# Which loads lie among the first MLP unit's weight tiles, and in which order its splits run: a decoder block on one core

## The chip, the core and the metric

One core of a Trainium2 chip runs one decoder block for 256 tokens of width 2048, in float32. The metric is the device time of one launch, in microseconds (us): the median of several runs.

## What is computed

The block is an adaptive-norm decoder layer. Six vectors of 2048 come from the conditioning vector and are used as shifts, scales and gates; two branches (a state-space one and an attention one) are merged, and an MLP follows. The end of it matters here:

```python
mod = silu(c) @ w_ada + b_ada                     # 12288 columns
sh1, sc1, g1, sh2, sc2, g2 = split(mod, 6)
...
x  = x + g1 * (merged @ w_out)
h2 = rms_norm(x, norm_mlp_g) * (1 + sc2) + sh2
x  = x + g2 * (square(relu(h2 @ w_ff1)) @ w_ff2)
return rms_norm(x, norm_final_g)
```

The weights (w_out 2048 x 2048, w_ff1 2048 x 8192, w_ff2 8192 x 2048, w_ada 2048 x 12288) are each read once.

## The kernel before, in words

**Products in three parts.** Every float32 weight tile (128 x 1024, 512 KB) is loaded into a raw buffer, `wraw`, of which there are seven, and then split in two: ScalarE (ACT in the profile) casts it to `hi` (line 137) and VectorE (DVE) computes `lo = raw - hi` (line 139). The activations are split in the same way. TensorE (PE) then does three matmuls for each product: hi by hi, hi by lo, lo by hi. There are four buffers each for `whi` and `wlo`; a few units write their splits into other large buffers that are free just then ("homes": `wVT`, `wQT` and so on). A raw buffer is free for the next load once VectorE has done the `lo` part.

**Engines and queues.** Each engine works through its own list in order, and all the loads concerned are issued by one queue, SyncE's (SP), in order as well. The order on each engine is set when the program is built, by a scheduler that goes by priorities and by extra edges: `self.after(ins)` puts what is issued inside it behind `ins`, when both are on the same engine. The lists `self.gates` and the values `self.gate` and `self.hgate` do this for the next weight tiles: an entry holds the instruction on VectorE behind which the `lo` part of a tile goes and the one on ScalarE behind which its cast goes. `turns` does it for matmuls: from a given tile on, the first product of a token half goes behind a given transpose.

**w_ada on VectorE.** Most of the product with w_ada isn't done on TensorE. A transposed tile of w_ada is loaded into a raw buffer (line 316), and VectorE multiplies it by the broadcast conditioning vector and sums it up (line 323, a "total"); after eight of these there are four columns' worth of 128 values. Such jobs wait in a lane, `ada`: after each weight tile that the program streams, the lane is credited its rate, and when a whole credit is there one job is issued (the load of one tile and the total of the one before). The constant `RM` is that rate for the section described next, and `self.agate`, when it is set, puts the totals behind the instruction it holds.

**The place of the change.** The second half of `w_out` (columns 1024 on) is done for tokens 0 to 127 first, then for tokens 128 to 255 ("halves" t = 0 and 1). Each half has its norm chain, `norm2(t)`: the gated result is added to x (lines 1159 and 1160), its squares are summed on ScalarE (line 1161), the sum goes through a square root on ScalarE (line 394) and a few one-column instructions on VectorE to the scaling of the row (line 1172, `xs`); TensorE transposes it (`trh`), ScalarE applies scale and shift (line 1193, `htmp`, one buffer), and the split makes `mh`. This is done for the two first quarters of the columns (c = 0 and 1) in turn; the other two follow later.

While the second half of the norm isn't done, the MLP starts with what there is. Four *units* (g = 0 to 3) form the products of the first half of the columns (K tiles 0 to 7) with 1024 columns of w_ff1 each, and keep them as `part`. The first unit, `gemm_h` with eight tiles, does all tiles for tokens 0 to 127 and then all for tokens 128 to 255, so that the second norm chain can run under the first; its tiles 4 to 7 go to `wVT` (two) and `wQT` (two). The units 1 to 3 are done in two runs of four tiles (`gemm_w`, 512 columns and two K tiles a load, line 179). Then the eight MLP groups follow (`ff1`, `ff2`), where the other K tiles are added.

Before the change, the lane's rate is 0.72 from the first unit on. The totals among the first unit's tiles are put behind `h1`, the last split of the second norm chain. The lo parts of tiles 1 to 3 go behind the first scaling of the first norm chain (`scaled[0]`), and the first half's matmuls of tile 7 go behind the second chain's last transpose.

Of the kernel before, what the change touches and what calls it, by code (L numbers as in the profile page):

```python
# [55 lines left out]
RSS = .43  # L56
RPA = .65
RWO = .45
RM = .72
NP = 4  # L60
TW = 9
TF = 3
# [12 lines left out]
class Kern:  # L75
# [776 lines left out]
    def body(self):  # L852
# [263 lines left out]
        for b in range(4):  # L1116
            t = sg[:, b]
# [53 lines left out]
            o, i_ = xs[:, t, c * 512:(c + 1) * 512], x1[:, t, c * 512:(c + 1) * 512]  # L1171
            return v.tensor_scalar(o, i_, rs2[t], None, op0=OP.mult)

        scaled = {}

        def norm2(t):
            add1(t)
            with self.hot():
                ss = self.col(f"ss2{t}", 1)
                self.pin(v.reduce_sum(ss, sq[:, 4 * t:4 * t + 4], axis=AX.X))  # L1180
                rs2[t] = self.rstd(ss, 1, f"r2{t}")
                tk = slice(t * P, (t + 1) * P)
                scaled[t] = [scale2(c, t) for c in range(2)][0]
                for c in range(2):
                    p = self.tmp("trh")
                    h = self.big.tile([P, 4, P], F32, name="htmp", tag="htmp", bufs=1)
                    for k in range(4):
                        kt = 4 * c + k
                        self.turned[2 * t + c] = nc.tensor.transpose(
                            p[:, k * P:(k + 1) * P], xs[:, t, kt * P:(kt + 1) * P], self.ident)  # L1190
                    for k in range(4):
                        kt = 4 * c + k
                        nc.scalar.activation(h[:, k], p[:, k * P:(k + 1) * P], AF.Identity,
                                             scale=A2[:, kt:kt + 1], bias=B2[:, kt:kt + 1])
                    last = self.split(mh[:, 4 * c:4 * c + 4, tk], ml[:, 4 * c:4 * c + 4, tk], h)
            return last

        norm2(0)
        next(parts)
        h1 = norm2(1)  # L1200
        self.agate = h1
        self.gates = [(None, None)] + [(scaled[0], None)] * 3

        g2b = self.slot("S3", [P, D], name="g2b")

# [80 lines left out]
                            final(t)  # L1286

        parts = []
        self.lanes["ada"][1] = RM
        for g in range(NP):  # L1290
            part = self.slot(("S4", "T", "SV", "S5")[g], [P, 8, S], name="part")
            if g == 0:
                halves = self.gemm_h(w1, range(0, 8), 0, mh, ml, self.homes(4, ("VT", "QT")), 8,
                                     turns=(((7, 3),), ()))
                for t in range(2):
                    banks = next(halves)
                    for b in (2 * t, 2 * t + 1):
# [5 lines left out]
                    v.tensor_add(part[:, 4 * i + b], part[:, 4 * i + b], banks[b][:, 0:S])  # L1303
            parts.append(part)
            if g == 0:
                self.agate = None
                self.gates = []
                with self.after(h1):
                    for c in (2, 3):
                        for t in range(2):  # L1310
# [61 lines left out]
```

## Time and profile before

| | us |
|---|---|
| median of 3 runs | 1423.72 |
| the three runs | 1422.74 to 1424.9 |
| the profiled execution, its own time | 1423.38 |
| its span, first to last instruction | 1421.6 |
| TensorE busy in the span | 1375.3 |
| VectorE busy | 1055.3 |
| ScalarE busy | 705.2 |

The granted clock of TensorE is 0.989 of full speed on average. A line of the timeline gives the start in us from the span's start, the duration, the engine, the line of the program, the operation and its output and inputs; in brackets stands for how long the engine was idle before it and what ended that. Matmuls are pipelined, so that starts lie closer together than the durations say. In a table by stage, "x" counts instructions, and the column behind the engines is TensorE's granted clock.

### The profile page before, as it was taken

The page shows a single profiled execution, that of the slowest core. Times are in us where ns is not written, and L with a number is a line of the kernel's source. Part 1 is how long each engine was busy: PE and PEld are TensorE (multiplying, and loading weights), DVE is VectorE, ACT ScalarE, POOL GpSimd, SP SyncE. Part 2 cuts the span into 40 slices and gives each one's busy share as a digit, 9 for nine tenths or more (in the row PEclk, how much of TensorE's full clock was granted, in tenths as well). Part 3 has the DMA queues.
Part 4 walks back from the last instruction along what each step waited for, and adds up shares of the span by engine and source line. Part 5 has one row for each costly group of instructions (what it writes and reads, how often), then busy time and mean ns, then how long its engine had stood idle before and what let it go on. Part 6 is the DMA issues. An engine that isn't in the chain of part 4 may idle for free.

```text
span 1421.6 us, 23396 instructions
## 1 busy us (share of the span) xinstructions
PE 1375.3 (97%) x9258; PEld 1222.9 (86%) x9258; DVE 1055.3 (74%) x1502; ACT 705.2 (50%) x937; POOL 40.9 (3%) x94
## 2 busy tenths in 40 slices
PE   7799999999999999999899999999999999999996
PEld 6789899899999999988678888888888888888885
DVE  5688999986799888978686675777666555555676
ACT  4444353357464853445555564545463544634444
POOL 1000000320000300000000000000000000000000
PEclk9899999999999999999999999999999999999998
DMA  8999987597457988797497577777767556465551
GB/s 336 353 385 348 314 306 244 164 286 251 150 189 250 309 315 295 285 349 283 160 320 246 186 260 250 235 254 292 251 220 267 184 188 194 175 208 190 181 205 61
DMA packets 113293, 353.19 MB, mean 248 GB/s; under 512 B 12080, under 2 KB 12096, under 8 KB 113056
## 3 DMA queue, kind: packets, MB, share of 16 engines
q1 hardware_dynamic: 110384, 347.13, 70.4%
q0 software_dynamic: 2800, 4.58, 1.1%
q8 instruction: 72, 1.18, 0.3%
q14 instruction: 37, 0.30, 0.1%
HBM read 347.27 MB, written 2.29 MB: 246 GB/s over the span
## 4 chain that ended last, share of the span: by engine, by line
PE 85%; DMA 6%; DVE 5%; ACT 2%; issue 2%; SPq 0%; DVEq 0%; ACTq 0%
PE pw L198 14%; PE pn L268 10%; PE pn L267 10%; PE pn L269 10%; PE pt L170 9%; PE pt L172 9%; PE pt L171 9%; PE pw L200 7%; DMA wraw<-in_w_in_dram 2%; DMA wraw<-in_w_ff_dram 2%; DVE wraw L323 2%; DVE wlo L139 1%; DMA wraw<-in_w_out_dram 1%; ACT whi L137 1%; PE ss L409 1%
## 5 line engine op out<-in xcount | busy, mean ns | idle before, releaser
L137 ACT CAST whi<-wraw 128x1024 fp32r<-128x1024 f32 x443 | 461.3, 1050 | 553.2 <-PE pn L268 179.9
L139 DVE TENSOR_TENSOR wlo<-wraw,whi 128x1024 fp32r<-128x1024 f32 x443 | 537.7, 1221 | 260.4 <-ACT whi L137 257.0
L198 PE MATMUL pw<-mh,whi 128*128 128x512 f32 x896 | 311.4, 396 | 1.6 <-ACT part L1298 0.7
L170 PE MATMUL pt<-ah,whi 128*128 128x256 f32 x896 | 252.2, 289 | 10.4 <-ACT whi L137 5.4
L171 PE MATMUL pt<-ah,whi 128*128 128x256 f32 x896 | 250.4, 285 | 0.0
L200 PE MATMUL pw<-mh,wlo 128*128 128x256 f32 x896 | 242.2, 280 | 2.3 <-DVE wlo L139 2.3
L172 PE MATMUL pt<-ah,wlo 128*128 128x256 f32 x896 | 239.1, 286 | 4.3 <-DVE wlo L139 4.2
L323 DVE SCALAR_TENSOR_TENSOR wraw<-wraw,cb 128x1024 f32<-128x1024 f32 x176 | 213.0, 1217 | 0.0
L268 PE MATMUL pn<-whi,ff 128*128 128x512 f32 x512 | 199.3, 389 | 0.0
L198 PEld LDWEIGHTS pw<-mh,whi 128*128 128x128 f32 x896 | 165.6, 188 | 38.3 <-ACT part L1298 1.1
L267 PE MATMUL pn<-whi,ff 128*128 128x512 f32 x512 | 198.4, 390 | 0.0
L170 PEld LDWEIGHTS pt<-ah,whi 128*128 128x128 f32 x896 | 172.3, 194 | 14.5 <-ACT whi L137 7.6
L269 PE MATMUL pn<-wlo,ff 128*128 128x512 f32 x512 | 184.6, 389 | 0.0
L200 PEld LDWEIGHTS pw<-mh,wlo 128*128 128x128 f32 x896 | 168.9, 188 | 7.6 <-DVE wlo L139 3.3
L171 PEld LDWEIGHTS pt<-ah,whi 128*128 128x128 f32 x896 | 172.8, 193 | 0.3
L172 PEld LDWEIGHTS pt<-ah,wlo 128*128 128x128 f32 x896 | 165.6, 193 | 6.2 <-DVE wlo L139 6.0
L267 PEld LDWEIGHTS pn<-whi,ff 128*128 128x128 f32 x512 | 96.1, 188 | 20.2 <-issue 0.2
L269 PEld LDWEIGHTS pn<-wlo,ff 128*128 128x128 f32 x512 | 96.0, 188 | 19.8
L268 PEld LDWEIGHTS pn<-whi,ff 128*128 128x128 f32 x512 | 96.2, 188 | 19.6
L1273 DVE TENSOR_TENSOR y<-y,pn 128x512 f32<-128x512 f32 x48 | 30.8, 682 | 14.1 <-PE pn L269 14.1
L267 PE MATMUL pn<-whi,mh 128*128 128x512 f32 x96 | 37.6, 392 | 0.0
L268 PE MATMUL pn<-whi,mh 128*128 128x512 f32 x96 | 37.4, 390 | 0.0
(400 smaller groups left out, 1657.4 us busy)
## 6 DMA issues: line engine op xcount, KB each, us to landing
wraw<-in_w_ff_dram SPq DMA_DIRECT2D x256, 512.0 KB, 4.8
wraw<-in_wat_dram SPq DMA_DIRECT2D x176, 512.0 KB, 5.7
wraw<-in_w_in_dram SPq DMA_DIRECT2D x128, 512.0 KB, 5.3
wraw<-in_w_out_dram SPq DMA_DIRECT2D x32, 512.0 KB, 6.3
wraw<-in_wan_dram SPq DMA_DIRECT2D x16, 512.0 KB, 8.5
wraw<-in_w_proj_attn_dram SPq DMA_DIRECT2D x16, 512.0 KB, 6.6
wraw<-in_w_proj_ssm_dram SPq DMA_DIRECT2D x16, 512.0 KB, 6.3
wraw<-in_w_glu_dram SPq DMA_DIRECT2D x8, 512.0 KB, 5.5
```

The costliest lines, as they stand in the source:

```text
L137: h = self.nc.scalar.copy(hi, src)
L139: s = self.nc.vector.tensor_sub(lo, src, hi.bitcast(F32))
L170: nc.tensor.matmul(o, hi[:, c], xh[:, kx, :], start=st, stop=False, skip_group_check=True)
L171: nc.tensor.matmul(o, hi[:, c], xl[:, kx, :], start=False, stop=False, skip_group_check=True)
L172: self.mm = nc.tensor.matmul(o, lo[:, c], xh[:, kx, :], start=False, stop=sp, skip_group_check=True)
L198: nc.tensor.matmul(banks[b], hi[:, c], x2[:, k0 + k].rearrange("p h s -> p (h s)"), start=i + k == 0, stop=False, skip_group_check=True)
L200: self.mm = nc.tensor.matmul(banks[b][:, 0:S], lo[:, c], x2[:, k0 + k, 0, :], start=False, stop=i == n - 1 and k == 1, skip_group_check=True)
L267: nc.tensor.matmul(o, xh[:, kx, tk], hi[:, c], start=q == 0, stop=False)
L268: nc.tensor.matmul(o, xl[:, kx, tk], hi[:, c], start=False, stop=False)
L269: self.mm = last = nc.tensor.matmul(o, xh[:, kx, tk], lo[:, c], start=False, stop=q == n - 1)
L323: v.scalar_tensor_tensor(w, w, 1.0, self.cb[:, (i % 2) * 1024:(i % 2 + 1) * 1024], op0=OP.mult, op1=OP.mult, accum_out=pc[:, i:i + 1])
L1273: v.tensor_add(d, d, banks[b])
```

## The change

Three numbers and two lists change, all within the section from the second norm to the fourth unit.

- The lane's rate is zero while the first unit's tiles are streamed, so that its eight loads follow one another. After the unit, six jobs of the lane are issued at once, with their totals behind `h1`; then the rate is 0.45 (before 0.72), so that ten more are spread over units 1 to 3.
- The gates of the first unit's tiles: the lo parts of tiles 1 to 5 go behind the first scaling of the first chain, and those of tiles 6 and 7 behind the last split of that chain (`h0`); the casts of tiles 3 to 7 go behind the first chain's square root (`roots[0]`).
- `turns`: the first half's matmuls go behind the second chain's last transpose from tile 6 on (before from tile 7 on).

```diff
-RM = .72
+RM = .45
...
-        scaled = {}
+        scaled, roots = {}, {}
...
                 rs2[t] = self.rstd(ss, 1, f"r2{t}")
+                roots[t] = self.sq_last
...
-        norm2(0)
+        h0 = norm2(0)
         next(parts)
         h1 = norm2(1)
-        self.agate = h1
-        self.gates = [(None, None)] + [(scaled[0], None)] * 3
+        self.gates = [(None, None)] + [(scaled[0], None)] * 2 + [(scaled[0], roots[0])] * 3 + [(h0, roots[0])] * 2
...
-        self.lanes["ada"][1] = RM
+        self.lanes["ada"][1] = 0.0
...
-                                     turns=(((7, 3),), ()))
+                                     turns=(((6, 3),), ()))
...
             if g == 0:
+                self.gates = []
+                self.agate = h1
+                for job in range(6):
+                    if self.lanes["ada"][0]:
+                        self.lanes["ada"][0].pop(0)()
                 self.agate = None
-                self.gates = []
+                self.lanes["ada"][1] = RM
```

What this moves is seen in the order of the instructions on each engine. Names carry a running number of the buffer's use. The first place is the loads on SyncE's queue, from the first unit's first tile on; before:

```order
L132 DMA wraw_7751<-in_w_ff1_dram 128x1024
L316 DMA wraw_7763<-in_wat_dram 128x1024
L132 DMA wraw_7766<-in_w_ff1_dram 128x1024
L132 DMA wraw_7778<-in_w_ff1_dram 128x1024
L316 DMA wraw_7790<-in_wat_dram 128x1024
L132 DMA wraw_7793<-in_w_ff1_dram 128x1024
L316 DMA wraw_7805<-in_wat_dram 128x1024
L132 DMA wraw_7808<-in_w_ff1_dram 128x1024
L132 DMA wraw_7819<-in_w_ff1_dram 128x1024
L316 DMA wraw_7829<-in_wat_dram 128x1024
L132 DMA wraw_7832<-in_w_ff1_dram 128x1024
L316 DMA wraw_7843<-in_wat_dram 128x1024
```

and now:

```order
L132 DMA wraw_7751<-in_w_ff1_dram 128x1024
L132 DMA wraw_7763<-in_w_ff1_dram 128x1024
L132 DMA wraw_7775<-in_w_ff1_dram 128x1024
L132 DMA wraw_7787<-in_w_ff1_dram 128x1024
L132 DMA wraw_7799<-in_w_ff1_dram 128x1024
L132 DMA wraw_7810<-in_w_ff1_dram 128x1024
L132 DMA wraw_7820<-in_w_ff1_dram 128x1024
L132 DMA wraw_7831<-in_w_ff1_dram 128x1024
L316 DMA wraw_7893<-in_wat_dram 128x1024
L316 DMA wraw_7896<-in_wat_dram 128x1024
L316 DMA wraw_7899<-in_wat_dram 128x1024
L316 DMA wraw_7902<-in_wat_dram 128x1024
```

The tiles of w_ff1 (line 132) stood two and one between w_ada tiles (line 316); now all eight come first and the w_ada tiles follow.

The second place is the first norm chain on ScalarE. `whi`, `wVT` and `wQT` are casts of the first unit's tiles, r20s is the square root, L1161 the squares; before:

```order
L137 CAST whi_7780<-wraw_7778 128x1024
L1161 ACTIVATE xs_6984,sq_6985<-x_6983 128x512 x2
L137 CAST whi_7795<-wraw_7793 128x1024
L394 ACTIVATE r20s_7609<-r20v_7608 128x1
L1193 ACTIVATE htmp_7620<-trh_7619,B2_115,A2_114 128x128 x4
L137 CAST mh_6424<-htmp_7620 128x4x128
L137 CAST wVT_7810<-wraw_7808 128x1024
L1193 ACTIVATE htmp_7632<-trh_7631,B2_115,A2_114 128x128 x4
```

and now (line 1194 is line 1193 before):

```order
L137 CAST whi_7777<-wraw_7775 128x1024
L1161 ACTIVATE xs_6984,sq_6985<-x_6983 128x512 x2
L394 ACTIVATE r20s_7609<-r20v_7608 128x1
L137 CAST whi_7789<-wraw_7787 128x1024
L137 CAST wVT_7801<-wraw_7799 128x1024
L137 CAST wVT_7801<-wraw_7810 128x1024
L137 CAST wQT_7822<-wraw_7820 128x1024
L1194 ACTIVATE htmp_7620<-trh_7619,B2_115,A2_114 128x128 x4
L137 CAST mh_6424<-htmp_7620 128x4x128
L137 CAST wQT_7822<-wraw_7831 128x1024
L1194 ACTIVATE htmp_7632<-trh_7631,B2_115,A2_114 128x128 x4
```

The root stood behind the cast of the fourth tile; now it stands ahead of it, and three more casts are done before the first chain's htmp.

On VectorE the same stretch, from the first chain's scaling to the second chain's add; before:

```order
L1172 TENSOR_SCALAR xs_6984<-x_6983,r20s_7609 128x512 x2
L139 TENSOR_TENSOR wlo_7769<-wraw_7766,whi_7768 128x1024
L139 TENSOR_TENSOR wlo_7781<-wraw_7778,whi_7780 128x1024
L139 TENSOR_TENSOR wlo_7796<-wraw_7793,whi_7795 128x1024
L139 TENSOR_TENSOR mh_6424<-htmp_7620,mh_6424 128x4x128
L139 TENSOR_TENSOR wVT_7810<-wraw_7808,wVT_7810 128x1024
L139 TENSOR_TENSOR wVT_7810<-wraw_7819,wVT_7810 128x1024
L139 TENSOR_TENSOR mh_6424<-htmp_7632,mh_6424 128x4x128
L1159 TENSOR_TENSOR xs_6984<-pn2_7351,g1b_7068 128x512
L1160 TENSOR_TENSOR x_6983<-x_6983,xs_6984 128x512
L1159 TENSOR_TENSOR xs_6984<-pn3_7352,g1b_7068 128x512
```

and now:

```order
L1172 TENSOR_SCALAR xs_6984<-x_6983,r20s_7609 128x512 x2
L139 TENSOR_TENSOR wlo_7766<-wraw_7763,whi_7765 128x1024
L139 TENSOR_TENSOR wlo_7778<-wraw_7775,whi_7777 128x1024
L139 TENSOR_TENSOR wlo_7790<-wraw_7787,whi_7789 128x1024
L139 TENSOR_TENSOR wVT_7801<-wraw_7799,wVT_7801 128x1024
L139 TENSOR_TENSOR wVT_7801<-wraw_7810,wVT_7801 128x1024
L139 TENSOR_TENSOR mh_6424<-htmp_7620,mh_6424 128x4x128
L139 TENSOR_TENSOR mh_6424<-htmp_7632,mh_6424 128x4x128
L1159 TENSOR_TENSOR xs_6984<-pn2_7351,g1b_7068 128x512
L139 TENSOR_TENSOR wQT_7822<-wraw_7820,wQT_7822 128x1024
L139 TENSOR_TENSOR wQT_7822<-wraw_7831,wQT_7822 128x1024
L1160 TENSOR_TENSOR x_6983<-x_6983,xs_6984 128x512
```

Five tile splits now stand between the scaling and the first `mh` split, where three did, and two more between the second chain's first multiply (L1159) and its add (L1160).

The third place is TensorE around the second chain's transposes, at the end of the first unit's first half; before:

```order
L229 MATMUL pn1_7748<-wVT_7810,mh_6424 128x512
L230 MATMUL pn1_7748<-wVT_7810,mh_6424 128x512
L228 MATMUL pn0_7747<-wQT_7834,mh_6424 128x512
L229 MATMUL pn0_7747<-wQT_7834,mh_6424 128x512
L228 MATMUL pn1_7748<-wQT_7834,mh_6424 128x512
L229 MATMUL pn1_7748<-wQT_7834,mh_6424 128x512
L230 MATMUL pn0_7747<-wQT_7834,mh_6424 128x512
L230 MATMUL pn1_7748<-wQT_7834,mh_6424 128x512
L1189 MATMUL trh_7716<-ident_85,xs_6984 128x128 x4
L1189 MATMUL trh_7728<-ident_85,xs_6984 128x128 x4
```

and now:

```order
L229 MATMUL pn1_7748<-wVT_7801,mh_6424 128x512
L230 MATMUL pn1_7748<-wVT_7801,mh_6424 128x512
L1190 MATMUL trh_7716<-ident_85,xs_6984 128x128 x4
L1190 MATMUL trh_7728<-ident_85,xs_6984 128x128 x4
L228 MATMUL pn0_7747<-wQT_7822,mh_6424 128x512
L229 MATMUL pn0_7747<-wQT_7822,mh_6424 128x512
L230 MATMUL pn0_7747<-wQT_7822,mh_6424 128x512
L228 MATMUL pn1_7748<-wQT_7822,mh_6424 128x512
L229 MATMUL pn1_7748<-wQT_7822,mh_6424 128x512
L230 MATMUL pn1_7748<-wQT_7822,mh_6424 128x512
```

The six matmuls of tile 6 (the first `wQT` tile) stood ahead of the transposes and now stand behind them. In units 1 to 3 on VectorE, a total (line 323) stood behind almost every split until the lane was empty, in the third unit's first run for instance as split, total, split, total, split, total; now it is split, total, split, split, total, and totals go on to the fourth unit.

## The prediction

> **What bounds the kernel now.** I read the page first, then the busy time by stage, then the chain of waits and the timelines of the stage that the edit touches. The page gives the span; the stages show where TensorE is not busy (columns: time, then PE, PEld, DVE, ACT, POOL busy, granted clock, DMA).
>
> ```profile
> span 1421.6 us, 23396 instructions
> 667.00:684.00 17.00, 14.88 (x71) 12.19 (x70) 13.96 (x24) 9.29 (x14) 0.00 (x0) 1.00 0.79 299
> 684.00:708.00 24.00, 21.95 (x90) 16.70 (x89) 14.52 (x24) 14.32 (x30) 0.00 (x0) 0.93 0.47 154
> 708.00:735.00 27.00, 25.61 (x139) 21.33 (x138) 25.90 (x43) 13.22 (x20) 0.00 (x0) 1.00 0.92 325
> 735.00:760.00 25.00, 22.43 (x126) 18.86 (x125) 17.38 (x26) 10.45 (x16) 0.00 (x0) 1.00 0.80 262
> 760.00:800.00 40.00, 40.00 (x232) 34.95 (x231) 23.43 (x33) 21.96 (x33) 0.00 (x0) 1.00 0.63 204
> ```
>
> TensorE is idle for 2.12 + 2.05 + 1.39 + 2.57 = 8.1 us between 667 and 760 and for nothing from 760 to 800: the stage from the second norm to the third MLP unit is the only one here with anything to win. Its idle ends, and the clock, in order:
>
> ```profile
> 680.23 0.39 PE L230 MATMUL pn<-wSV,mh 128*128 128x512 f32 x1
> 682.73 1.07 PE L1189 MATMUL trh<-ident,xs 128*128 128x128 f32 x8 [2.12 <-DVE xs L1172]
> 683.55 0.49 PE L228 MATMUL pn<-wS,mh 128*128 128x512 f32 x1
> 683.50:687.20 3.70, 3.70 (x12) 0.55 0.51 151
> 689.37 0.62 PE L228 MATMUL pn<-whi,mh 128*128 128x512 f32 x2
> 698.43 0.61 PE L230 MATMUL pn<-wQT,mh 128*128 128x512 f32 x2
> 699.97 1.06 PE L1189 MATMUL trh<-ident,xs 128*128 128x128 f32 x8 [0.92 <-DVE xs L1172]
> 701.14 0.50 PE L228 MATMUL pn<-wQT,mh 128*128 128x512 f32 x1
> 704.09 0.73 PE L228 MATMUL pn<-whi,mh 128*128 128x512 f32 x2 [0.96 <-ACT mh L137]
> 704.82 0.50 PE L229 MATMUL pn<-whi,mh 128*128 128x512 f32 x1
> 715.38 0.84 PE L198 MATMUL pw<-mh,whi 128*128 128x512 f32 x3
> 716.87 0.50 PE L198 MATMUL pw<-mh,whi 128*128 128x512 f32 x1 [0.65 <-ACT part L1298]
> 744.58 0.39 PE L200 MATMUL pw<-mh,wlo 128*128 128x256 f32 x1 [1.03 <-DVE wlo L139]
> 746.06 0.50 PE L198 MATMUL pw<-mh,whi 128*128 128x512 f32 x1 [0.51 <-DVE part L1303]
> 757.85 0.39 PE L200 MATMUL pw<-mh,wlo 128*128 128x256 f32 x1 [1.03 <-DVE wlo L139]
> ```
>
> Two things are to be seen. From 680.62 to 683.55 no matmul runs (2.93 us, the transposes apart), and the next 3.7 us run at a clock of 0.55; from 699.04 to 701.14 none runs either (2.10 us), and the clock stays. And the chain of waits through this unit goes over loads of w_ff1 tiles, because w_ada tiles, which are held until the second half's norm chain ends, take the raw buffers:
>
> ```profile
> 684.20 3.35 DMA wraw<-in_w_ff_dram
> 689.90 4.31 DMA wraw<-in_w_ff_dram
> 696.58 3.44 DMA wraw<-in_w_ff_dram
> ```
>
> **The change, part by part.** Sums are against the profiled execution, 1423.38 us (its span and 1.8 us around it); the median of the three runs, 1423.72, lies 0.34 above it. The rows of VectorE (DVE) and ScalarE (ACT) that carry the working:
>
> ```profile
> 679.78 0.16 DVE L1180 TENSOR_REDUCE ss<-sq 128x1 f32<-128x4 f32 x1 [1.01 <-ACT xs L1161]
> 682.10 0.88 DVE L1172 TENSOR_SCALAR xs<-x,r20s 128x512 f32<-128x512 f32 x2
> 682.90 3.49 DVE L139 TENSOR_TENSOR wlo<-wraw,whi 128x1024 fp32r<-128x1024 f32 x3
> 693.23 0.68 DVE L1159 TENSOR_TENSOR xs<-pn,g1b 128x512 f32<-128x512 f32 x1
> 697.94 0.16 DVE L1180 TENSOR_REDUCE ss<-sq 128x1 f32<-128x4 f32 x1 [0.79 <-ACT xs L1161]
> 699.34 0.88 DVE L1172 TENSOR_SCALAR xs<-x,r21s 128x512 f32<-128x512 f32 x2
> 704.07 0.69 DVE L139 TENSOR_TENSOR mh<-htmp,mh 128x512 fp32r<-128x512 f32 x1 [1.73 <-ACT mh L137]
> 707.60 1.22 DVE L323 SCALAR_TENSOR_TENSOR wraw<-wraw,cb 128x1024 f32<-128x1024 f32 x1
> 743.32 1.21 DVE L139 TENSOR_TENSOR wlo<-wraw,whi 128x1024 fp32r<-128x1024 f32 x1
> 744.46 1.21 DVE L323 SCALAR_TENSOR_TENSOR wraw<-wraw,cb 128x1024 f32<-128x1024 f32 x1
> 680.13 1.05 ACT L137 CAST whi<-wraw 128x1024 fp32r<-128x1024 f32 x1 [0.38 <-DMA wraw<-in_w_ff_dram]
> 683.40 1.51 ACT L1193 ACTIVATE htmp<-trh,B,A 128x128 f32<-128x128 f32 x4 [2.12 <-PE trh L1189]
> 684.94 0.62 ACT L137 CAST mh<-htmp 128x512 fp32r<-128x512 f32 x1
> 697.19 0.63 ACT L1161 ACTIVATE xs<-x 128x512 f32<-128x512 f32 x1 [1.27 <-DVE x L1160]
> ```
>
> *First norm chain.* Before, the cast at 680.13 (1.05) stands on ScalarE ahead of the root, and from the sum of squares to the scaling takes 2.32 us (679.78 to 682.10); the second chain, with no cast between, takes 1.40. The root now stands ahead of that cast: 0.92 less. The two casts ahead of the squares read tiles that are loaded one place earlier: some 0.2 more. Scaling at 680.95, transposes 0.63 later (682.10 to 682.73) at 681.6, first matmul at 682.4. The gap without matmul is then 1.8 us, below the 2.10 that kept the clock. The next 18 matmuls took 5.82 us (683.55 to 689.37); at the pitch of the 40 from 689.37 to 698.43, 0.2265, they take 4.08: TensorE stands at the unit's first tile at 686.5, 2.9 us early.
>
> *That is taken back at once.* The added gates put five tile splits on VectorE between this scaling and the first transposed half's split (three before). At 1.14 each (3.49 for three, overlap taken off) they run from 681.75 to 687.5, and the 0.69 split ends at 688.2. TensorE needs it two matmuls after 686.5 and waits 1.25 us. All five tiles are there: eight loads in a row have no w_ada tile among them, and none is waited for. So this wait is VectorE's own work; were a tile late, the price would be the lateness.
>
> *Second norm chain.* There is one htmp buffer, so the next four ACTIVATEs start at 688.2: 1.51, cast 0.62, split 0.69, at 691.05. Then on VectorE the gated multiply (L1159), two splits of 1.14, which the order puts inside the chain, and the three other instructions of 0.68: to 695.9. From the last square's start to the sum 0.75 (697.19 to 697.94), 1.40, 0.63: transposes at 698.7, against 699.97. Before, this chain stood behind splits whose tiles waited for buffers (the three loads above); those waits go, but the splits that now run ahead of it and in it use most of the gain up.
>
> *The turn.* Six matmuls (1.36 us) now stand behind these transposes and not ahead. TensorE does 34 matmuls from 688.2 to 695.9, the last ends at 696.1, and the next matmul is at 698.7 + 0.82 = 699.5: 3.4 us without one. The nearest gap is that of 2.93, not that of 2.10, so I take the clock as lost: 3.7 us with nine matmuls in them (as from 683.55 on), the other three at the pitch, end at 703.95. The other half's first split is ready at 698.7 + 0.67 + 1.51 + 0.62 + 0.69 = 702.2, so the wait of 0.96 and the 0.3 more up to 704.82 are gone. From here on **0.4 us** is won (1.8 more if the clock holds). The Trainium skill, in "TensorE: Matmul & The Clock Gate", section "Part 1: The HAM clock gate", states that the clock is halved after an idle window of about 3.4 us, counted by a window that runs freely. By that figure alone a gap of 3.4 us lies on the edge, and the sum could as well be that of the held clock, below. The trace puts the loss lower, after 2.93 us, and the row decides.
>
> *Start of the second unit.* The chain's end is at 705.7 (702.2, then 1.51, copy 0.59, cast and split), against 707.68. The six held w_ada totals (1.14 each) start there, and each frees the buffer for one load, so loads are 2 us earlier for a TensorE that is 0.4 us earlier. The bank's copy waits for the second tile's cast and is then in time: **0.65** won.
>
> *Units two to four.* Ten totals over 24 tiles stand where ten stood over the first fourteen or so. In the third unit a total lay between each pair of splits; the third split ran at 743.32 and TensorE waited 1.03. Now the second and third are neighbours, and the third ends 1.14 earlier: enough. Its cover is that thin: one total more in front and the 1.03 is back. Where a total still stands ahead of the bank's adds, I leave 0.6 in one half unit and 0.1 elsewhere. The waits there are 1.03 + 0.51 + 1.03 and 0.74 (1.39 less 0.65) of the earlier stage, 3.3 in all: **2.6** won. Bounds: none of it, if the totals meet the splits elsewhere, to all 3.3. The last w_ada columns are now ready at about 775, not 760; the last tile that needs them comes about 2 us after their split, and beyond that each us costs one.
>
> The moves on SyncE's queue cost nothing by themselves: five w_ada loads are issued behind the unit's tiles, and hold buffers that no tile wants before the first total frees one; the second unit's loads are queued behind them, as behind the held ones before. Sum: 0.4 + 0.65 + 2.6 = **3.65 us**; 1423.72 - 3.65 = **1420.1**.
>
> **The rivals.**
>
> - *The clock holds over the second gap.* Gain 0.4 + 1.8 = 2.2, the bank's wait of some 0.55 comes back, the rest as above: 4.8, or 1418.9. For it: one gap of 2.10 was harmless; against: 2.93 was not. By the freely running window of the Trainium skill's page above, a gap near its length may or may not be seen; no run here shows that yet.
> - *The later units keep their waits.* VectorE is 96% busy from 708 to 735 (25.90 of 27) and 70% after; the totals that now reach to the fourth unit find its tightly timed splits. Then 0.4 + 0.65 remain: 1422.7. Against: the stage 760:800 has no idle at VectorE 59%, and ten totals (11.4 us) over the 70 us to about 785 add 16%.
> - *The second chain waits for the eighth tile.* Its load starts only when the first gated split ends (about 683.0), and its split now stands inside the norm chain. It lands 3.4 us later (684.20's row), its cast ends at 687.4, and it is wanted at 692.75: 5.3 us of cover. Past that, each us goes to the end, the gain is eaten at 3.65 more, and at some 11.8 us of lateness the kernel is 2.85 slower: 1426.6 or more. The longest of the three loads is 4.31.
> - *Nothing reaches the end:* what is won in the stage is lost in ff1 behind it: 1423.7. Against it: TensorE has no idle there that could take it up.
>
> **How the numbers follow.** A measurement of this kernel can tell some 0.2%, 2.85 us, from no change: the border is 1420.87. The forecast has 0.50 (of it 0.10 above the border, when half a wait more stays), the held clock 0.17, kept waits 0.21, no effect 0.05, the late tile 0.07. Faster: 0.40 + 0.17 = 0.57. Same: 0.10 + 0.21 + 0.05 = 0.36. Slower: 0.07. The range goes from the held clock with every later wait gone (2.2 + 0.1 + 3.3 = 5.6 under, 1418.1) to the case without effect (1423.7); outside are the slower case and some of the edges.
>
> **What would show it.** Transposes of the first half at about 681.6 with the clock whole after them; a wait of about 1.2 us for a VectorE split at the unit's first tile; 2.6 us of idle ahead of the second transposes and then about 3.5 us at half clock; no wait for a bank at the second unit; about 0.7 us of idle in units two to four. A whole clock there, or waits over 2 us in those units, would make the forecast wrong.

## The result, and the profile after

| | median, us | runs | lowest to highest |
|---|---|---|---|
| before | 1424.31 | 4 | 1422.74 to 1425.26 |
| after | 1415.51 | 4 | 1414.18 to 1417.49 |

The ratio is 0.9945, with an interval of 0.9933 to 0.9958: the change makes the kernel 8.8 us faster, where 3.65 were forecast. A second comparison with more runs gave 0.9952 (0.9940 to 0.9964), 1423.45 to 1416.42. Over all comparisons below, the kernel before has a median of 1423.29 in 53 runs and the changed one of 1415.38 in 11: 7.9 us. The profiled execution of after took 1415.01.

From the page of after, the span:

```profile
span 1412.9 us, 23391 instructions
```

and the busy time of after in the stages that were shown of before, by the same columns (time, then PE, PEld, DVE, ACT, POOL busy, granted clock, DMA):

```profile
667.00:684.00 17.00, 16.38 (x77) 13.33 (x75) 15.62 (x25) 13.01 (x20) 0.00 (x0) 1.00 0.75 281
684.00:708.00 24.00, 20.53 (x94) 16.62 (x93) 15.16 (x28) 10.03 (x24) 0.00 (x0) 1.00 0.45 160
708.00:735.00 27.00, 26.80 (x156) 23.23 (x156) 23.08 (x36) 16.98 (x26) 0.00 (x0) 1.00 0.88 318
735.00:760.00 25.00, 24.49 (x139) 20.88 (x138) 16.87 (x26) 11.68 (x18) 0.00 (x0) 1.00 0.77 256
760.00:800.00 40.00, 39.72 (x226) 34.53 (x227) 27.73 (x45) 21.23 (x32) 0.00 (x0) 1.00 0.73 245
```

TensorE's idle time from 708 to 760 has fallen from 1.39 + 2.57 us to 0.20 + 0.51. From 684 to 708 it has grown, from 2.05 to 3.47, but the clock there is whole now, where it was 0.93. From 760 to 800 there are now 0.28. TensorE's timeline of after shows both:

```profile
677.66 0.39 PE L230 MATMUL pn<-wSV,mh 128*128 128x512 f32 x1
678.66 1.06 PE L1190 MATMUL trh<-ident,xs 128*128 128x128 f32 x8 [0.62 <-DVE xs L1172]
679.49 0.47 PE L228 MATMUL pn<-wS,mh 128*128 128x512 f32 x1
...
683.69 0.61 PE L228 MATMUL pn<-whi,mh 128*128 128x512 f32 x2
...
685.25 0.50 PE L229 MATMUL pn<-whi,mh 128*128 128x512 f32 x1 [0.94 <-DVE mh L139]
...
692.86 0.39 PE L230 MATMUL pn<-wVT,mh 128*128 128x512 f32 x1
695.78 1.06 PE L1190 MATMUL trh<-ident,xs 128*128 128x128 f32 x8 [2.53 <-DVE xs L1172]
696.60 0.48 PE L228 MATMUL pn<-wQT,mh 128*128 128x512 f32 x1
...
699.43 0.62 PE L228 MATMUL pn<-whi,mh 128*128 128x512 f32 x2
...
710.31 0.85 PE L198 MATMUL pw<-mh,whi 128*128 128x512 f32 x3
...
711.57 0.50 PE L198 MATMUL pw<-mh,whi 128*128 128x512 f32 x1 [0.20 <-ACT part L1298]
...
749.22 0.50 PE L198 MATMUL pw<-mh,whi 128*128 128x512 f32 x1 [0.51 <-DVE part L1303]
...
803.61 0.39 PE L267 MATMUL pn<-whi,mh 128*128 128x512 f32 x1
```

From 693.25 to 696.60 no matmul runs (3.35 us), and the twelve that follow up to 699.43 take 2.83 us, at full pitch. The first line shows something else: the last matmul ahead of everything that the change moves ends a stage whose order is the same in both kernels, yet stands at 677.66, against 680.23 in the trace of before. These 2.57 us of the 8.7 between the two spans lie ahead of the change. So all traces are compared from this matmul on, "the place". The offsets from it to the first matmul of the second unit (L198), to the first of the part behind the four units (L267), and to the end of the span:

| trace | the place | second unit | behind the units | end | clock falls behind the place |
|---|---|---|---|---|---|
| before | 680.23 | 35.15 | 132.11 | 741.37 | first gap |
| before, again | 680.47 | 36.24 | 135.19 | 744.43 | first gap, second unit |
| after | 677.66 | 32.65 | 125.95 | 735.24 | none |
| after, again | 679.44 | 33.04 | 126.40 | 735.66 | none |
| after, third | 677.81 | 32.65 | 125.46 | 734.69 | none |
| after, fourth | 677.64 | 32.72 | 125.52 | 734.76 | none |
| gates and turn only | 676.27 | 34.54 | 130.32 | 739.53 | second gap |
| loads only | 677.82 | 36.45 | 131.06 | 740.28 | first gap, twice as long |
| rate as before | 681.22 | 32.69 | 126.77 | 735.98 | none |
| rate only | 676.87 | 35.38 | 128.34 | 737.63 | first gap |
| turn 7 | 679.97 | 32.70 | 126.63 | 735.93 | none |
| turn 5 | 677.56 | 35.46 | 127.65 | 736.84 | second gap |
| splits after chains | 681.57 | 33.29 | 126.48 | 735.73 | second gap |
| splits after chains, 2 | 680.09 | 29.90 | 124.50 | 733.71 | none |

The place itself moves by 5.3 us (676.27 to 681.57) over executions whose order on TensorE is the same up to there. The last column leaves out the fall in the last 10 us of the span, which every trace has. From the place to the end the change wins 6.13 us between the first two traces: 2.50 up to the second unit, 3.66 in the units, nothing behind them. By the means of two traces of before and four of after it is 7.8 (742.9 to 735.1): 2.9, 4.9 and nothing. That agrees with the 7.9 of the medians, though the two traces of before lie 3.06 us apart.

### The profile page after: what moved, and what is told of

It is laid out like the page before. It is cut to its first block, busy times and chain, and to the rows that moved or that the text cites. A ratio compares the mean times of both kernels' runs of the same rounds, so it can differ in the third digit from the quotient of the medians.

```text
span 1412.9 us, 23391 instructions
## 1 busy us (share of the span) xinstructions
PE 1370.8 (97%) x9258; PEld 1221.4 (86%) x9258; DVE 1054.7 (75%) x1502; ACT 705.7 (50%) x937; POOL 40.8 (3%) x94
## 5 line engine op out<-in xcount | busy, mean ns | idle before, releaser
L198 PE MATMUL pw<-mh,whi 128*128 128x512 f32 x896 | 311.3, 396 | 1.0 <-DVE part L1303 0.5
L267 PE MATMUL pn<-whi,ff 128*128 128x512 f32 x512 | 198.6, 390 | 0.0
L198 PEld LDWEIGHTS pw<-mh,whi 128*128 128x128 f32 x896 | 165.4, 188 | 37.3 <-DVE part L1303 0.8
L267 PEld LDWEIGHTS pn<-whi,ff 128*128 128x128 f32 x512 | 96.1, 188 | 20.1 <-issue 0.2
L267 PE MATMUL pn<-whi,mh 128*128 128x512 f32 x96 | 37.6, 392 | 0.0
```

The lines of the kernel that those rows point to most:

```text
L198: nc.tensor.matmul(banks[b], hi[:, c], x2[:, k0 + k].rearrange("p h s -> p (h s)"), start=i + k == 0, stop=False, skip_group_check=True)
L267: nc.tensor.matmul(o, xh[:, kx, tk], hi[:, c], start=q == 0, stop=False)
```

## The experiments

**The same kernels again.** Nothing is edited; the runs ask what belongs to the change and what to the execution.

> The changed kernel once more, nothing edited. Theory A: some 6.1 us of the gain are made between the second norm and the last w_ada column, and the other 2.6 us, by which the profiled execution after already stood earlier at the last matmul ahead of the changed place (677.66 against 680.23), are chance in the kernel's first 70 us; then that matmul falls anywhere from 677 to 681 in other executions, and the ratio with more rounds comes out nearer to 0.9957 (1418.2) than to 0.9945. Rival B: the earlier start belongs to the changed program; then the matmul stands at 677.7 to within 0.3 again, and the ratio stays at 0.994. On the second gap without a matmul (3.35 us before the second half's transposes are through): theory A, the clock stays whole at that length in each execution; rival C, it is a matter of phase, and in some execution the next 3.7 us run at about 0.55 and cost 1.8 us.

Median 1416.42 in 5 runs, ratio 0.9952 (0.9940 to 0.9964). The place stood at 679.44, so rival B falls, and the stretch behind it took 735.66. The ratio lies between the two theories', and its interval holds both; the medians are 7.0 us apart, where theory A has 6.1. The clock stayed whole.

> The kernel before once more, nothing edited, for its time from the last matmul ahead of the changed place (680.23 in the first trace) to the end of the span. Theory A: that stretch is 741.4 us again, to within 0.5, and the kernel before differs between executions by the place of that matmul alone (676.3 to 681.2 in the traces so far). Rival F: the stretch itself varies, since the clock is lost over the first gap or not, and over the second (2.1 us) too in some executions; then it lies between 739.5 and 743.5, and the change's gain in the medians (7 to 8 us) is larger than that of the two first traces (6.1) because the first trace of before was a lucky one.

The stretch took 744.43, beyond rival F's range, and 3.06 more than in the first trace. TensorE's timeline of this second execution of before:

```profile
683.16 1.94 PE L1189 MATMUL trh<-ident,xs 128*128 128x128 f32 x8 [2.31 <-DVE xs L1172]
...
705.43 0.73 PE L228 MATMUL pn<-whi,mh 128*128 128x512 f32 x2 [0.96 <-ACT mh L137]
...
731.68 0.49 PE L198 MATMUL pw<-mh,whi 128*128 128x512 f32 x1 [0.47 <-ACT whi L137]
...
733.38 0.38 PE L200 MATMUL pw<-mh,wlo 128*128 128x256 f32 x1 [1.20 <-DVE wlo L139]
```

Here the clock fell at 683.07, just ahead of the first transposes, which took 1.94 us instead of 1.07, and again in the second unit, where a wait for a cast is followed by one for a split. Theory A is wrong on this point: the kernel before varies behind the place as well, and its first trace was the better of the two.

**The parts of the change.** The gates and the turn alone, on the old lane:

```diff
-        self.gates = [(None, None)] + [(scaled[0], None)] * 3
+        self.gates = [(None, None)] + [(scaled[0], None)] * 2 + [(scaled[0], roots[0])] * 3 + [(h0, roots[0])] * 2
-                                     turns=(((7, 3),), ()))
+                                     turns=(((6, 3),), ()))
```

> Only the gates and the turn of the change; w_ada tiles among the first unit's tiles as before, rate .72. The root now stands ahead of the cast, so the first gap without a matmul is about 1.8 us and the clock stays whole behind it (theory A: transposes 1.1 us earlier against the place's own start, 2.9 us won at the unit's first tile). Theory A: nearly none of it reaches the end, because the second norm chain still stands behind splits whose tiles wait for buffers; and as six matmuls fewer stand ahead of its transposes, the gap there grows from 2.1 to 5 us or more and the clock is lost there: 1424 to 1426, no gain. Rival D: the gates carry the change, the loads only help the later units: 1419 to 1421.

Median 1420.47 in 11 runs, ratio 0.9984 (0.9975 to 0.9992); 739.53 from the place. The first gap without a matmul was 1.88 us and kept the clock; the second was 4.43 and lost it, as theory A said. But the median lies in rival D's range: against the two traces of before, 0.6 and 1.7 us are won up to the second unit (34.54 against 35.15 and 36.24), and in the units, which took 95.78, 1.2 and 3.2. Theory A had priced the clock right and the gates too low; but the change isn't carried by them.

The loads alone (the six jobs after the unit, rate 0 and then .45; gates and turn as before):

```diff
-        self.gates = [(None, None)] + [(scaled[0], None)] * 2 + [(scaled[0], roots[0])] * 3 + [(h0, roots[0])] * 2
+        self.gates = [(None, None)] + [(scaled[0], None)] * 3
-                                     turns=(((6, 3),), ()))
+                                     turns=(((7, 3),), ()))
```

> Only the loads of the change (eight w_ff1 tiles in a row, six held w_ada jobs behind them, rate .45 afterwards), gates and turn as before. The order puts three splits of 1.14 us into the first norm chain. Theory A: the scaling comes 2 to 3 us later than in the changed kernel, the first gap without a matmul is 4 to 5 us and the clock is lost behind it (3.7 us at about 0.55, 1.7 us lost), while VectorE has fewer splits left ahead of the second chain; the units behind are as in the changed kernel: 1418 to 1421, 1 to 3 us of the gain lost. Rival D: the gates carry it: 1423 or more.

Median 1420.46 in 10 runs, ratio 0.9981 (0.9969 to 0.9993); 740.28 from the place. The gap was 6.51 us and the clock was low for 6.83, both more than expected; the second unit started at 36.45, later than in either trace of before. With the loads free, splits run into the first norm chain; the gates keep them out. VectorE's timeline has three of them ahead of the first scaling:

```profile
678.02 1.22 DVE L139 TENSOR_TENSOR wVT<-wraw,wVT 128x1024 fp32r<-128x1024 f32 x1 [1.44 <-ACT wVT L137]
...
679.58 1.22 DVE L139 TENSOR_TENSOR wVT<-wraw,wVT 128x1024 fp32r<-128x1024 f32 x1
...
680.79 1.20 DVE L139 TENSOR_TENSOR wQT<-wraw,wQT 128x1024 fp32r<-128x1024 f32 x1
...
682.49 0.88 DVE L1172 TENSOR_SCALAR xs<-x,r20s 128x512 f32<-128x512 f32 x2
```

Against the mean of before (742.9) the gates win 3.4 and the loads 2.6, the whole change 7.8. This run also has the lower rate in the later units. Beside the run of that rate alone, below (737.63), it is 2.65 slower: without the gates the eight loads in a row lose time, and with them they win it.

The rate, and the rate alone:

```diff
-RM = .45
+RM = .72
```

> The changed kernel with the rate of w_ada jobs in units two to four back at .72. Theory A: the totals stand between neighbouring splits again, and 1 to 2.6 of the 3.3 us of waits in these units come back: 1417 to 1419 beside a changed kernel at 1416 to 1418. Rival E: the waits went because the first unit ends earlier and its buffers come free earlier, whatever the rate: no difference from the changed kernel, within 0.5 us in the traces.

Median 1417.99 in 6 runs, ratio 0.9965 (0.9953 to 0.9976). The units take 94.08 us (126.77 less 32.69) against 93.07 in the mean of the changed kernel's four traces: 1.0 comes back, the lower end of theory A. But it isn't the waits that theory A names: the third unit's waits for a split, 1.03 and 1.03 before, stay away. What came back is a wait at the second unit's bank, with 0.52 more in the third unit:

```profile
716.92 0.50 PE L198 MATMUL pw<-mh,whi 128*128 128x512 f32 x1 [1.18 <-ACT part L1298]
```

The kernel before, with this line where its first unit ends:

```diff
                 self.gates = []
+                self.lanes["ada"][1] = .45
```

> The kernel before with the rate of w_ada jobs at .45 from the end of the first unit on; first unit as before. It asks what the spreading of the totals is worth without the first unit's part. Theory A: VectorE's totals are what holds the third and fourth units up, so their waits of 1.03, 0.51 and 1.03 us shrink to one of 0.5, and the 1.2 us wait at 733 of the second trace of before, which cost it the clock, goes too: 1.5 to 2.5 us won, 739 to 740 us from the place where the first unit's code begins to the end, median 1421 to 1422. Rival E: the waits went because the first unit ended 2.5 us earlier, and its buffers with it: 0 to 0.5 us won, 741 to 744 us, median 1423 to 1424.

Median 1418.79 in 6 runs, ratio 0.9969 (0.9957 to 0.9981). The second unit starts at 35.38, as before, and the units take 92.96 us, against 96.96 and 98.95 before: 4.0 and 6.0 won, more than either theory had. TensorE's waits in this trace:

```profile
679.56 1.09 PE L1189 MATMUL trh<-ident,xs 128*128 128x128 f32 x8 [2.30 <-DVE xs L1172]
...
696.75 1.07 PE L1189 MATMUL trh<-ident,xs 128*128 128x128 f32 x8 [0.87 <-DVE xs L1172]
...
700.96 0.73 PE L228 MATMUL pn<-whi,mh 128*128 128x512 f32 x2 [0.96 <-ACT mh L137]
...
739.52 0.50 PE L198 MATMUL pw<-mh,whi 128*128 128x512 f32 x1 [0.46 <-DVE part L1303]
```

The three waits of the first unit are those of before, and in the units one of 0.46 is left. So the rate alone does all that the change does in the units, and what the rest of the change adds to it is 2.5 us (737.63 against 735.09), all up to the second unit. Rival E is wrong in its "no difference", but has a part: with the first unit changed, the old rate costs 1.0 and not 4.0, and the waits for splits are gone at either rate.

**The second gap.** The turn is the dose: how many matmuls stand ahead of the second half's transposes.

```diff
-                                     turns=(((6, 3),), ()))
+                                     turns=(((7, 3),), ()))
```

> The changed kernel with the turn back at 7: six matmuls (1.36 us) stand ahead of the second half's transposes again, so the gap without a matmul there is about 2.0 us and not 3.35. Theory A (the clock held over 3.35 us): nothing changes, the stretch from the last matmul ahead of the changed place to the end stays at 735.2 to 735.7 us, within 0.3; median 1416 to 1416.5. Rival C (the clock over the second gap is a matter of phase and was lost in some of the unprofiled executions): 0.5 to 1 us better in the median, 1415 to 1415.5. Third possibility: the six matmuls ahead of the transposes wait for the second split of the seventh tile's weights: 0.2 to 0.5 slower.

Median 1417.62 in 6 runs, ratio 0.9959 (0.9945 to 0.9974); 735.93 from the place. The gap was 2.00 us, the clock whole, and a wait of 0.82 for the other half's cast came back behind it. The time is 0.8 over the mean of the changed kernel (735.09), more than the third possibility has and with another wait, but only 0.27 over the slowest of its four traces, within theory A's margin: one trace doesn't decide between them. The median isn't lower, so rival C gets nothing from it.

```diff
-                                     turns=(((6, 3),), ()))
+                                     turns=(((5, 3),), ()))
```

> The changed kernel with the turn at 5: six more matmuls stand behind the second half's transposes, so the gap without a matmul there grows from 3.35 to about 4.7 us. Theory A, with what the gates and turn alone showed (4.43 us without a matmul, then 3.3 us at a clock of 0.5): the clock is lost, 1.7 us later to the end, 737 us from the last matmul ahead of the changed place, median 1417.7 to 1418.2. Rival G: it is not the length of the gap but the state of VectorE and the loads that made the clock fall there; then as the changed kernel, 735.5 and 1416.3.

Median 1419.24 in 12 runs, ratio 0.9970 (0.9960 to 0.9981); 736.84 from the place, 1.75 over the changed kernel. The gap was 5.44 us and the clock fell: theory A. The median lies some 1 us above its range, however, and 3.9 over the changed kernel's; the trace doesn't show why.

**Where the clock falls.** In all traces the falls and rises of the clock within an execution lie on a grid. Stretches of the first trace of before (time, PE busy, clock, DMA):

```profile
21.71:28.53 6.82, 6.35 (x36) 0.50 1.01 404
264.05:267.47 3.42, 3.42 (x72) 0.50 0.85 264
680.48:683.89 3.41, 1.29 (x11) 1.00 0.04 16
683.89:687.31 3.42, 3.42 (x10) 0.50 0.58 171
```

From 21.71 to 264.05 there are 71 steps of 3.4132 us, to 683.89 there are 194 of 3.4133; each spell of low clock is one step, or two, or three, but for the one that the record ends in. The program doesn't set the grid: its edges stand at another place of the program in each execution. They don't stand just anywhere, though: in all fourteen traces an edge falls between 15.82 and 17.69 us behind the place, on little more than half of a step. What decides the clock of a step, as far as these traces show it, is how busy TensorE was in the step before. The third row is such a step, with 1.29 us of work, and the fourth follows at half clock. The step ahead of the fall in the second unit, in the second execution of before:

```profile
730.85:734.27 3.42, 1.62 (x8) 1.00 1.00 376
734.27:737.68 3.41, 3.41 (x10) 0.50 0.96 332
```

and the two steps over the second gap in the first execution of after:

```profile
691.53:694.94 3.41, 1.72 (x8) 1.00 0.75 268
694.94:698.35 3.41, 2.57 (x16) 1.00 0.02 10
```

An edge at 694.94 cut the idle time in two, and 1.72 us of work on one side were enough. Of the steps between 660 and 800 us, all those at full clock with 1.62 us of work or less were followed by half clock, and none with 1.70 or more. The transposes count as work in this. In the trace with the old rate a step with 0.96 us of matmuls and 0.82 of transposes kept the clock:

```profile
697.72:701.13 3.41, 1.78 (x12) 1.00 0.19 78
```

Steps at about 160 us, named at the end, lost the clock with more work than that, so the border of some 1.65 us is one of this part of the kernel.

> The changed kernel a third time, for the clock alone. In the ten traces so far every fall and rise of the clock within one execution lies on a grid of 3.413 us, which stands elsewhere against the program in each. Theory A2 (the clock falls at an edge of this grid when TensorE was busy for less than about 1.65 of the 3.41 us ahead of it: 1.62 and less fell between 660 and 800 us, 1.72 and more held): whether the second gap costs the clock hangs on where the grid lies. If one stretch of the grid holds 1.76 us or more of the 2.5 us of idle ahead of the second transposes, the clock falls and 1.7 us are lost: about 737.1 us from the last matmul ahead of the changed place. If an edge cuts the idle time nearer to its middle, it holds: 735.2 to 735.7. Rival C2: a gap of 3.35 us never costs the clock, wherever the grid lies: 735.2 to 735.7 in any case.

> The changed kernel a fourth time; as for the third: theory A2, the clock falls behind the second gap if and only if one stretch of the execution's own 3.413 us grid holds 1.76 us or more of the idle time ahead of the second transposes (then 737.1 us to the end, otherwise 735.2 to 735.7); rival C2, it holds wherever the grid lies.

The third took 734.69 and the fourth 734.76, with the clock whole. The fourth's steps over the gap:

```profile
691.63:695.04 3.41, 1.70 (x8) 1.00 0.73 258
695.04:698.45 3.41, 2.62 (x16) 1.00 0.04 16
```

In neither did a step hold 1.76 us of the idle time, so both theories expected what came, and these two runs don't tell them apart. The other kernels do: gaps of 2.93 us (before), 3.12 (rate only) and 3.42 (splits after chains) lost the clock, and gaps of 3.05 (before, again) and 3.31 to 3.36 (five traces) kept it. Length alone doesn't order them, nor does the idle time in them (2.12 us in before lost the clock, 2.50 to 2.54 in the changed kernel kept it); the work in the grid's steps does. That the changed kernel itself loses the clock when the grid lies badly follows from this, but no trace shows it.

**VectorE's order in the first unit.** What is left there are 0.94 us at the first tile and 2.53 ahead of the second transposes. VectorE's timeline of after:

```profile
678.83 3.49 DVE L139 TENSOR_TENSOR wlo<-wraw,whi 128x1024 fp32r<-128x1024 f32 x3
682.24 2.35 DVE L139 TENSOR_TENSOR wVT<-wraw,wVT 128x1024 fp32r<-128x1024 f32 x2
684.51 0.69 DVE L139 TENSOR_TENSOR mh<-htmp,mh 128x512 fp32r<-128x512 f32 x1
...
688.09 0.68 DVE L1159 TENSOR_TENSOR xs<-pn,g1b 128x512 f32<-128x512 f32 x1
688.69 2.35 DVE L139 TENSOR_TENSOR wQT<-wraw,wQT 128x1024 fp32r<-128x1024 f32 x2
690.96 0.68 DVE L1160 TENSOR_TENSOR x<-x,xs 128x512 f32<-128x512 f32 x1
...
695.15 0.88 DVE L1172 TENSOR_SCALAR xs<-x,r21s 128x512 f32<-128x512 f32 x2
```

Two splits stand ahead of the first quarter's split (684.51), two between a multiply of the second chain and its add. Moved behind (`mids[0]` is the first quarter's split, `self.added` the second chain's last add):

```diff
-        self.gates = [(None, None)] + [(scaled[0], None)] * 2 + [(scaled[0], roots[0])] * 3 + [(h0, roots[0])] * 2
+        self.gates = [(None, None)] + [(scaled[0], None)] * 2 + [(scaled[0], roots[0])] + [(mids[0], roots[0])] * 2 + [(self.added, roots[0])] * 2
```

> The changed kernel with two gates moved: the two wVT splits stand behind the split of the first transposed quarter (not ahead of it), the two wQT splits behind the last add of the second chain (not between its multiply and its add). Theory A (VectorE's order is what still holds TensorE up in the first unit): the wait of 0.94 us at the unit's first tile goes, the second chain starts some 1.2 us earlier and has 2.35 us less inside it; its transposes come about 2.7 us earlier, and the 2.53 us of idle ahead of them shrink to under 1: 2 to 2.6 us won, 733 us from the last matmul ahead of the changed place, median 1413.5 to 1414.5. Rival H: the late wQT splits now hold TensorE up behind the transposes, or the totals that follow are pushed into the second unit: 0 to 1 us won, 1415.5 to 1416.5.

Median 1416.60 in 6 runs, ratio 0.9954 (0.9938 to 0.9970); 735.73 from the place: the number of rival H, though not its reason. The wait at the first tile went, but the second transposes came only 1.0 us earlier (17.16 from the place, 18.12 in after), since the two splits still stood between the last add and the sum of squares, and the clock fell there:

```profile
695.74:699.15 3.41, 1.19 (x8) 1.00 0.53 186
699.15:702.57 3.42, 3.42 (x12) 0.50 0.31 122
```

So one of the two goes behind the second scaling, and the last tile's cast behind the first half's last cast:

```diff
-... + [(mids[0], roots[0])] * 2 + [(self.added, roots[0])] * 2
+... + [(mids[0], roots[0])] * 2 + [(self.added, roots[0]), (scaled[1], cast0)]
```

> As the run with splits behind the chains, but only one wQT split behind the last add, the other behind the second scaling, and the cast of the last wQT tile behind the first half's last cast. There the two splits (2.35 us) still stood between the last add (693.83) and the sum of squares (696.71), and the cast (688.04 to 689.09) ahead of the ACTIVATEs. Theory A: the sum comes 1.2 us earlier by the one split and up to 0.9 by the cast; the transposes stand 15.2 to 16 us behind the last matmul ahead of the changed place (17.16 there, 18.12 in the changed kernel), the idle time ahead of them is under 1.2 us and can no longer cost the clock: 733 to 734.3 us to the end, median 1414 to 1415.5, under the changed kernel's. Rival H: what is won at the transposes is lost to the late split of the last wQT tile or at the second unit: 735 to 736.

Median 1413.70 in 5 runs, ratio 0.9931 (0.9918 to 0.9943): the lowest median of all, 1.7 us under the changed kernel's 1415.38. The intervals of the two ratios overlap, and the two single runs of the changed kernel in the same comparison took 1414.46 and 1414.43, so the size of this gain is not settled. TensorE's timeline:

```profile
680.09 0.39 PE L230 MATMUL pn<-wSV,mh 128*128 128x512 f32 x1
...
695.44 1.06 PE L1191 MATMUL trh<-ident,xs 128*128 128x128 f32 x8 [0.50 <-DVE xs L1173]
...
725.54 0.39 PE L200 MATMUL pw<-mh,wlo 128*128 128x256 f32 x1 [0.33 <-DVE wlo L139]
```

The transposes stand 15.35 us behind the place and 0.50 of idle is left. The second unit starts 2.9 us earlier than in the changed kernel (29.90 against 32.77), of which 1.4 reach the end (733.71 against 735.09): the units take 94.60 us instead of 93.07.

## Why the prediction was wrong

The direction was right, and the largest terms but one had the right mechanism; the time lay 2.6 us below the range. Point by point, in offsets from the place:

- *First norm chain: right.* Transposes were forecast 1.37 us behind the place (681.6) and came at 1.00 to 1.38; the unit's first tile at 6.27, measured 6.03 to 6.42. The clock behind the first gap held in each trace of the changed kernel (gaps of 1.44 to 1.82 us).
- *Taken back by the splits: right, a third too large.* A wait of 1.25 us for VectorE was forecast; it was 0.93 to 0.94, and no tile was late.
- *Second chain: right.* 18.47 forecast, 18.12 to 18.51 measured. A gap of 3.4 us was forecast, and it was 3.31 to 3.36.
- *The turn: the step that failed.* "The nearest gap is that of 2.93, not that of 2.10, so I take the clock as lost." It held in four traces of four. With the 1.8 us that this step took off, 2.2 would have stood where 2.50 were measured up to the second unit (first traces). The fault was to read one gap that lost the clock as a length that loses it. What counted in 2.93 us was that a single step of the grid took nearly all of it (1.29 us of work in 3.41); a longer gap cut by an edge does less. The trace of before could have shown it: its edge at 683.89, carried on by four steps of 3.413, gives one at 697.54, in the middle of the idle time that was forecast from 696.1 to 698.7. The Trainium skill, in "TensorE: Matmul & The Clock Gate", section "Part 1: The HAM clock gate", gives a free-running window of 3413 ns; the grid of 3.413 us agrees with it. Its condition of an idle window is stricter than what is seen here: 1.62 us of work in a step did not prevent the fall, and the runs decide. The prediction had the free-running window in a rival with 0.17. How much more it deserved is less plain. With the edges anywhere at equal odds, the border of 1.65 us would lose the clock over this gap in some seven cases of ten (an estimate from the matmul times of the first trace of after). In the four traces an edge fell 16.85 to 17.41 us behind the place, and cut the idle time ahead of the transposes (from about 15.6 to 18.1) so that at most 1.71 us of it lay on one side. Why the edges keep so near is not shown, and that the clock held each time may be luck in part.
- *Start of the second unit and units two to four: right, too small.* 0.65 + 2.6 = 3.25 were forecast; 3.66 were won between the first traces, and 4.9 by the means. The idle time there fell from 3.96 to 0.99 us (0.20 for the bank, 0.51, and 0.28 at 794.68). The reason given, totals between neighbouring splits, agrees with the rate alone: 4.0 with nothing else changed. That these waits also go at the old rate, once the first unit is changed, it did not foresee.
- *The base: wrong by some 1.5 us, unseen.* All was counted against one execution of before. Its stretch behind the place (741.37) was the better of two (744.43), as waits of the second unit can cost that kernel the clock a second time. With the mean of the two (742.9) the whole change is worth 7.8 and not 6.1. One trace can't show this; the waits next to each other at 731.31 and 732.52 could have been a warning.

The turn alone doesn't explain the miss: the end of the range already has the clock held and every later wait gone, 2.2 up to the second unit and 0.1 + 3.3 in the units. By the means 2.9 and 4.9 were won. The first comparison, with four runs of each kernel, gave 8.8; more runs give 7.9, near the 7.8 of these means.

In the units the idle time fell by 2.97 between the first traces, and 3.66 were won. Part of the other 0.7 is that the prediction took each wait at its bracket, which counts from the modelled end of the matmul before. In before:

```profile
742.82 0.40 PE L198 MATMUL pw<-mh,whi 128*128 128x512 f32 x1
743.05 0.28 PE L200 MATMUL pw<-mh,wlo 128*128 128x256 f32 x1
743.16 0.39 PE L198 MATMUL pw<-mh,whi 128*128 128x512 f32 x1
744.58 0.39 PE L200 MATMUL pw<-mh,wlo 128*128 128x256 f32 x1 [1.03 <-DVE wlo L139]
```

The last two start 1.42 us apart, where the first two start 0.23 apart: the wait costs 1.19 and not 1.03.

Of the rivals, the held clock was the nearest, at 1418.9. It had the mechanism, and it too lay 3.4 us over the result, for the reasons just given. The late eighth tile didn't happen: its cast waited 0.59 us for the load, until 683.64, and its split is the second of the two from 688.69 on. The later units didn't keep their waits.

What stays open: how often the changed kernel loses the clock over its second gap (four traces of four did not), and why the place moves by 5.3 us. Most of that arises early: six hundred matmuls into the kernel TensorE already stands anywhere from 101.2 to 106.2 us. Spells of low clock ahead of it differ between executions (from 21.71 and from 42.19 in the first trace of before), but no run was made to separate them from the loads there.

## What to carry to other kernels

Compare two traces from the last instruction that both kernels have in common, and take a second trace of the kernel before: what lies ahead of that point, and what the second trace does otherwise, is no effect of the change. A gap in TensorE's work isn't to be judged by its length against one gap that cost the clock; lay the execution's own 3.41 us grid over it (the trace of before has one), and where the grid can't be known, keep both outcomes, or make the gap so short that no step can hold enough of it. And work that VectorE does for later tiles is better put behind a norm chain than inside it: moving splits out of the chains won 1.4 us more in the one trace of it. Spreading the totals over more tiles won 4 us alone. A change of several parts should be taken apart: the loads in a row were worth having only together with the gates.

## What the runs showed of the hardware

- The clock's edges lie on a grid of 3.413 us that the program doesn't set; the low clock lasts whole steps (3.41, 6.83 or 10.24 us), but for the spell in which the record ends.
- A step can lose the clock though TensorE works through almost half of it: 1.62 of 3.42 us did, 1.70 of 3.41 did not, between 660 and 800 us. Elsewhere the border lies otherwise: at 160.72 of the second trace of after, a step with 1.95 us of work was followed by half clock, at 160.86 of splits after chains, 2, one with 2.04.
- Transposes count as work for the clock (0.96 us of matmuls and 0.82 of transposes kept it) and slow down with it: eight of them took 1.94 us where the clock had fallen ahead of them, and 1.06 otherwise.
